# Hybrid SSD and Conformer layer: latent convolution in 32x32 tiles, layer norm by channels, decay rows on ScalarE's queue

## The chip, the cores and the metric

One Trainium2 core runs the whole program in one launch. Its engines work side by side and meet at semaphores: TensorE (PE, with PEld for its weight loads), VectorE (DVE), ScalarE (ACT), GpSimd (POOL) and SyncE (SP), which here only issues DMA transfers. The metric is the device time of one execution in microseconds (us).

## What is computed

One trunk layer is applied to 256 context tokens and to 2048 latent tokens (a grid of 32 rows by 64 columns), 1024 wide. After an RMS norm with a modulation, one projection gives all branches. The part that the change touches:

```python
h = ga * jax.nn.sigmoid(gb)
h = depthwise_conv(h, conv_w, conv_b)      # 31 taps along the grid's rows axis, per channel
h = layer_norm(h, ln_g, ln_b)              # over the 1024 channels of a token
y_conf = jax.nn.silu(h) * jax.nn.silu(gsil)
y_ssd = rms_norm((y_f + y_b + d * xs) * jax.nn.silu(z), norm_g)   # two scans, chunks of 128
out = jnp.concatenate([y_ssd, y_conf], -1) @ w_out
y = x + gate * rms_norm(out, g_post)
```

On the latent grid the convolution runs over the 32 rows for each of the 64 columns and each channel, so for one channel it is a 32x32 banded (Toeplitz) matrix times a 32x64 image. On the context it runs over 256 tokens.

## The kernel before

Activations are kept channel-major for the projection: 128 channels on partitions, tokens along the free axis. Float32 products of the projections are made of three passes of rounded halves (lines 378 to 380: high by high, low by high, high by low), 24 matmuls of 512 columns for one output bank of a block of 512 tokens. Three PSUM banks (`mm`) take these outputs in turn; five (`ss`) serve everything small. The 2304 tokens are worked in two halves (ten and eight tiles of 128 tokens). Each half first does the SSD inputs with their short convolution (`xbc_unit`), then `post`: the gated Conformer product (`gab_unit`, stored to DRAM as `GL`, channel-major), then the silu gates (`silu_unit`, stored to `ZS` and `GS`). Beside `post` runs a list of generators, `scan` and `extra`, which `interleave` and `merge` step at a fixed rate between the projection's matmuls.

- `scan` (`pass_a`, 18 tiles of 128 tokens) is the forward SSD scan. `load_lb` (line 664) loads rows of cumulated decays, spread over all partitions; POOL masks them (676), ACT takes the exponential (673, 684), DVE mixes the two directions (688, 689), and PE applies them (720). Each direction has four such buffers.
- `extra` in the second half holds the convolutions. `ctx_conv` does the context with 31 DVE steps, two PE transposes and a store to `CVC`. `lat_conv` does 128 latent channels: `kd` receives the banded taps, `x` the input, each in four loads. Four channels share one matmul: the partitions are 4 channels by 32 rows, and `expand` (line 622, ACT) writes the four 32x32 bands on the diagonal of a 128x128 weight. Channels are taken in eight groups of 128, and for each of them come four blocks of eight products (line 634), each block with one `ss` bank and one DVE instruction (639) that adds the bias. The result is stored token-major to `CVL` (644).

The last stage does the output projection, one tile of 128 tokens after another in the order 17 down to 2, then 1, 0. In tile i, 96 matmuls of 512 columns (`out_part`, line 1078) multiply the SSD half (`yh`, k = 0 to 7) and the Conformer half (`ph`/`pl`, k = 8 to 15) with `w_out`. Between them stand the preparations of later tiles. `ssd_pre` closes the backward scan for the tile after next (16 matmuls, 985) and squares it (989, 991). `ssd_norm` sums over the channels by a matmul with ones (1004), takes the root on POOL (135), and `ssd_scale` spreads it over the partitions by another matmul (1012, 1013). `conf_pre` loads the convolution token-major and takes mean and variance with DVE's statistics (1042 to 1047); `conf_act` transposes it back by eight PE transposes (1058), and applies the affine and silu on ACT (1061) and the gate on DVE (1063). `conf_hl` splits it in halves (1069, 1070). `finish` normalises the output, adds x and stores it.

The order of instructions on each engine is not simply that of the code: a planner replays the program with its own costs and, on each engine, takes the next instruction that its replay finds ready, by the order in the code. The result is fixed before the run. All DMA transfers are issued from SP's queue, in order, and a transfer that has to wait for a buffer holds those behind it.

Of the kernel before, what the change touches and what calls it, by code (L numbers as in the profile page):

```python
# [8 lines left out]
F32 = mybir.dt.float32  # L9
# [58 lines left out]
def backbone_kernel(ctx, tc, xa, xt_in, cols, rows, wconv, conf_b, gp_row, bg_row, state0, w_mod, w_dt, w_in, w_out,  # L68
# [19 lines left out]
    CVC = dram("cvc", [NCTX * P, D])  # L88
    CVL = dram("cvl", [LAT, D])
# [437 lines left out]

    def gab_unit(half, j, hb):
        wb = next_w()
        wa = next_w()  # L530
        for b in ORDER[half]:
# [48 lines left out]
    def ctx_conv(j, tile):  # L580
# [22 lines left out]
    def lat_conv(j, lp, kbuf):  # L603
        cbb = lp.tile([P, HD], F32, tag="cbb", name=f"cbb{j}", bufs=2)
        for h in range(2):
            c0 = j * P + h * 64
            DMA.dma_start(cbb[h * 64:(h + 1) * 64], conf_b[c0:c0 + 64].partition_broadcast(64))
        kd = lp.tile([P, 32, 32], F32, tag="kd", name=f"kd{j}", bufs=1)
        for c4 in range(4):
            src = bass.AP(tensor=wconv.tensor, offset=(j * 4 + c4) * 64 * 32, ap=[[32, 32], [1, 1024]])  # L610
            DMA.dma_start(kd[c4 * 32:(c4 + 1) * 32].rearrange("p r g -> p (r g)"), src)

        x = lp.tile([P, 32, 64], F32, tag="cx", name=f"cx{j}", bufs=1)
        src = GL[j][:, 256:].rearrange("(g c) (r w) -> c r g w", c=4, w=64)
        for c4 in range(4):
            DMA.dma_start(x[c4 * 32:(c4 + 1) * 32], src[c4])

        def expand(u):
            kt = kbuf[u % 2]
            for c4 in range(4):  # L620
                rs = slice(c4 * 32, (c4 + 1) * 32)
                S.copy(kt[rs, :, rs].rearrange("p (h q) r -> p h q r", h=2),
                       kd[rs].rearrange("p r (h u q) -> p u h q r", h=2, u=4)[:, u])

        vt = lp.tile([P, 32, HD], F32, tag="cvv", name=f"cvv{j}", bufs=1)
        yield
        expand(0)
        yield
        for u in range(4):
            kt = kbuf[u % 2]  # L630
            ps = bank("ss", f"cp{j}_{u}")
            for q in range(4):
                for h in range(2):
                    T.matmul(ps[h * 64:(h + 1) * 64, q * P:(q + 1) * P], x[:, h * 16 + u * 4 + q, :], kt[:, h * 4 + q, :],
                             start=True, stop=True)
            if u < 3:
                expand(u + 1)
            yield
            V.scalar_tensor_tensor(vt[:, ::-1, u * 16:(u + 1) * 16].rearrange("p r c -> p c r"),
                                   ps.rearrange("p (c r) -> p c r", r=32), 0.5,  # L640
                                   cbb[:, u * 16:(u + 1) * 16].unsqueeze(2).to_broadcast([P, 16, 32]), MUL, ADD)
        for h in range(2):
            c0 = j * P + h * 64
            DMA.dma_start(CVL[:, c0:c0 + 64].rearrange("(r w) c -> w r c", w=64), vt[h * 64:(h + 1) * 64])
        yield


    def pass_a(i):
# [11 lines left out]
        def load_lb(g, hq):  # L660
            for d in range(2):
                lb = pa.tile([P, 4, P], F32, tag=f"lb{d}", name=f"lb{i}{g}{hq}{d}", bufs=4)
                r0 = il * 32 + d * NH + g * 8 + hq * 4
                DMA.dma_start(lb.rearrange("p h l -> p (h l)"),
# [264 lines left out]
    kbuf = [lp.tile([P, 8, P], F32, name=f"kbuf{u}") for u in range(2)]  # L929
    for u in range(2):  # L930
        G.memset(kbuf[u], 0.0)
    blocks = post(1, 5)
    cg = lambda name: lp.tile([P, D], F32, tag="cg", name=name, bufs=2)
    extra = chain(f for j in range(4) for f in (lat_conv(2 * j, lp, kbuf), ctx_conv(j + 4, cg), lat_conv(2 * j + 1, lp, kbuf)))
# [32 lines left out]

    def ssd_pre(i, first):
# [21 lines left out]
        zr = p1.tile([P, P], F32, tag="zr", name=f"zr{i}", bufs=2)  # L990
        V.tensor_reduce(zr, z.rearrange("p q l -> p l q"), mybir.AxisListType.X, ADD)
# [9 lines left out]
    def ssd_norm(i, yz):  # L1001
        y, zr = yz
        pm = bank("ss", f"pm{i}")
        T.matmul(pm[:, 0:1], zr, ones[:, 0:1], start=True, stop=True)
        ms = p1.tile([P, 1], F32, tag="ms", name=f"yms{i}", bufs=2)
        V.tensor_scalar(ms, pm[:, 0:1], 1.0 / D, 4.0 * EPS, MUL, ADD)
        r = rstd_of(p1, ms, f"yr{i}")
        return y, r, pm

    def ssd_scale(i, yrp):  # L1010
        y, r, pm = yrp
        T.matmul(pm[:, P:2 * P], r.to_broadcast([P, P]), ident, start=True, stop=True)
        V.tensor_tensor(y, y, pm[:, P:2 * P].unsqueeze(1).to_broadcast([P, 8, P]), MUL)
        return ssd_hl(i, y)
# [22 lines left out]
    def conf_pre(i):  # L1037
        n = p2.tile([P, D], F32, tag="cn", name=f"cn{i}", bufs=1)
        DMA.dma_start(n, CVC[i * P:(i + 1) * P, :] if i < 2 else CVL[(i - 2) * P:(i - 1) * P, :])
        bs = p2.tile([P, 12], F32, tag="bs", name=f"bs{i}", bufs=2)  # L1040
        for h in range(2):
            V.bn_stats(bs[:, 6 * h:6 * h + 6], n[:, h * 512:(h + 1) * 512])
        mv = p2.tile([P, 2], F32, tag="mv", name=f"mv{i}", bufs=2)
        V.bn_aggr(mv, bs)
        V.tensor_scalar(mv[:, 1:2], mv[:, 1:2], EPS, None, ADD)
        r = rstd_of(p2, mv[:, 1:2], f"cr{i}")
        V.tensor_scalar(n, n, mv[:, 0:1], r, SUB, MUL)
        return n

    def conf_act(i, n):  # L1050
        gs = p2.tile([P, 8, P], F32, tag="gs", name=f"gsl{i}", bufs=1)
        DMA.dma_start(gs, chan_slice(GS, i))
        v = p2.tile([P, 8, P], F32, tag="v", name=f"v{i}", bufs=1)
        for g in range(2):
            ps = bank("ss", f"ct{i}{g}")
            for c in range(4):
                k = 4 * g + c
                T.transpose(ps[:, c * P:(c + 1) * P], n[:, k * P:(k + 1) * P], ident)
            for c in range(4):
                k = 4 * g + c  # L1060
                S.activation(v[:, k, :], ps[:, c * P:(c + 1) * P], AF.Silu, bias=cv[:, C_LNB + k:C_LNB + k + 1],
                             scale=cv[:, C_LNG + k:C_LNG + k + 1])
# [47 lines left out]
    gap(wo2, 64)  # L1110
# [8 lines left out]
    for b in range(2):  # L1119
        for n, u in enumerate(last):  # L1120
            run(take(u, 8))
            if b == 0 and n == 1:
                yr = ssd_norm(i, yz)
            if b == 1 and n == 0:
# [105 lines left out]
```

## Time and profile before

| | |
|---|---|
| time, median of 3 runs | 1878.53 us (1878.14 to 1878.75) |
| the profiled execution | 1882.2 us, its span 1880.5 us |
| granted TensorE clock | 0.986 of full speed |
| PE busy | 1825.6 us (97%) |
| DVE, ACT, POOL busy | 63%, 45%, 14% |
| DMA | 375.29 MB, 200 GB/s |

A group of the profile reads: line, engine, operation, output <- inputs, shape, count, then busy time in us and mean ns of one, then the idle time of that engine just before, with what ended it. Where a line is one of the timeline or of the chain of waits, it begins with its start in us. Float32 matmuls without the split into halves appear as two instructions each. A matmul's length contains its passage through the array; what one costs in a series is the distance between starts.

### The profile page before, as it was taken

What the parts mean: (1) busy time and instruction counts of PE and PEld (TensorE: products, weight loads), DVE (VectorE), ACT (ScalarE), POOL (GpSimd) and SP (SyncE); (2) the same over time, 40 slices, a digit from 0 to 9 for tenths busy, and PEclk for the clock granted to TensorE, in tenths of its full rate; (3) what the DMA queues carried; (4) which work ended last, traced back from release to release, by engine and by line L of the source; (5) the groups of instructions that cost most, each with busy time, mean ns of one, the idle gap of its engine ahead of it and who ended that gap; (6) DMA issues with size and microseconds to landing.
All of it is one profiled execution on the core that took longest, in us unless ns stands there. A gap on an engine that the chain in (4) does not pass through costs nothing.

```text
span 1880.5 us, 26833 instructions
## 1 busy us (share of the span) xinstructions
PE 1825.6 (97%) x9739; PEld 1504.6 (80%) x9739; DVE 1188.2 (63%) x1699; ACT 839.5 (45%) x1786; POOL 269.0 (14%) x351
## 2 busy tenths in 40 slices
PE   7899999999999999999999899999999999999998
PEld 4788887787887888888877677777887888888887
DVE  2477887776545553577585768655427676766662
ACT  3646424443455441644355666675414232232321
POOL 0002001111111100100001011110013333333220
PEclk9899999999999999999999999999999999999999
DMA  8556575564677754545587897978887655555532
GB/s 302 212 200 198 211 239 179 176 222 155 211 269 225 225 200 169 165 154 188 179 195 215 210 242 194 278 185 234 239 268 239 191 174 173 165 172 173 175 102 78
DMA packets 290400, 375.29 MB, mean 200 GB/s; under 512 B 85206, under 2 KB 187478, under 8 KB 290268
## 3 DMA queue, kind: packets, MB, share of 16 engines
q1 hardware_dynamic: 290268, 373.58, 64.2%
q8 instruction: 77, 1.26, 0.3%
q14 instruction: 55, 0.45, 0.1%
HBM read 243.92 MB, written 129.59 MB: 199 GB/s over the span
## 4 chain that ended last, share of the span: by engine, by line
PE 62%; DMA 5%; ACT 3%; issue 3%; DVE 2%; SPq 2%; POOL 0%; POOLq 0%; DVEq 0%; ACTq 0%
PE op L1078 20%; PE sp L378 6%; PE sp L379 6%; PE sp L380 6%; DMA lb<-lt 3%; PE xp L379 2%; PE xp L378 2%; PE xp L380 2%; PE py L720 2%; PE ga L378 2%; PE ga L380 1%; PE po L727 1%; PE ga L379 1%; PE qo L985 1%; PE gb L378 1%
## 5 line engine op out<-in xcount | busy, mean ns | idle before, releaser
L684 ACT ACTIVATE lb<-lb,WB 128x128 f32<-128x128 f32 x576 | 184.1, 391 | 150.9 <-POOL lb L676 149.0
L378 PE MATMUL sp<-hh,wh 128*128 128x512 f32 (+1 forms) x640 | 239.7, 375 | 2.6 <-DVE sth L550 2.6
L379 PE MATMUL sp<-hl,wh 128*128 128x512 f32 (+1 forms) x640 | 237.0, 370 | 0.0
L380 PE MATMUL sp<-hh,wl 128*128 128x512 f32 (+1 forms) x640 | 236.7, 370 | 0.2 <-DMA wl<-wld 0.2
L676 POOL TENSOR_SCALAR_AFFINE_SELECT lb<-lb 128x512 f32<-128x512 f32 x144 | 108.7, 760 | 749.7 <-ACT el L673 416.1
L378 PE MATMUL xp<-hh,wh 128*128 128x512 f32 (+1 forms) x480 | 179.1, 375 | 6.1 <-ACT wh L353 4.0
L379 PE MATMUL xp<-hl,wh 128*128 128x512 f32 (+1 forms) x480 | 179.1, 373 | 0.2 <-DVE hl L299 0.2
L380 PE MATMUL xp<-hh,wl 128*128 128x512 f32 (+1 forms) x480 | 179.2, 374 | 0.0
L475 DVE SCALAR_TENSOR_TENSOR cva<-raw,cwh,cva 128x1280 f32<-128x1280 f32 (+1 forms) x96 | 142.7, 1495 | 15.5 <-ACT cva L469 13.6
L378 PEld LDWEIGHTS sp<-hh,wh 128*128 128x128 f32 x640 | 121.0, 189 | 24.3 <-DVE sth L550 3.1
L380 PEld LDWEIGHTS sp<-hh,wl 128*128 128x128 f32 x640 | 121.0, 189 | 21.6 <-DMA wl<-wld 0.7
L379 PEld LDWEIGHTS sp<-hl,wh 128*128 128x128 f32 x640 | 121.2, 189 | 20.1 <-issue 0.5
L378 PE MATMUL gb<-hh,wh 128*128 128x512 f32 (+1 forms) x320 | 121.9, 381 | 3.4 <-DVE gth L539 3.4
L378 PE MATMUL ga<-hh,wh 128*128 128x512 f32 (+1 forms) x320 | 120.4, 376 | 2.6 <-ACT gth L536 2.6
L379 PE MATMUL gb<-hl,wh 128*128 128x512 f32 (+1 forms) x320 | 119.3, 373 | 0.0
L380 PE MATMUL gb<-hh,wl 128*128 128x512 f32 (+1 forms) x320 | 119.1, 372 | 0.0
L380 PE MATMUL ga<-hh,wl 128*128 128x512 f32 (+1 forms) x320 | 118.1, 369 | 0.0
L379 PE MATMUL ga<-hl,wh 128*128 128x512 f32 (+1 forms) x320 | 117.9, 369 | 0.0
L590 DVE SCALAR_TENSOR_TENSOR cg<-cg,cv 128x256 f32<-128x256 f32 x240 | 113.3, 497 | 2.5
L550 DVE SCALAR_TENSOR_TENSOR sth<-sth,sp 128x512 f32<-128x512 f32 (+1 forms) x80 | 50.4, 630 | 98.4 <-ACT sth L549 98.4
L378 PEld LDWEIGHTS xp<-hh,wh 128*128 128x128 f32 x480 | 92.0, 192 | 23.0 <-ACT wh L353 4.8
L688 DVE TENSOR_TENSOR lb<-lb,lb 128x512 f32<-128x512 f32 x72 | 51.6, 717 | 85.6 <-ACT lb L684 55.8
(219 smaller groups left out, 3860.8 us busy)
## 6 DMA issues: line engine op xcount, KB each, us to landing
lb<-lt SPq DMA_DIRECT2D x144, 256.0 KB, 4.2
wr<-in_w_in SPq DMA_DIRECT2D x88, 256.0 KB, 4.9
whd<-wh SPq DMA_DIRECT2D x44, 512.0 KB, 3.4
wld<-wl SPq DMA_DIRECT2D x44, 512.0 KB, 4.7
wh<-whd SPq DMA_DIRECT2D x44, 512.0 KB, 5.2
wl<-wld SPq DMA_DIRECT2D x44, 512.0 KB, 5.6
xT<-xb SPq DMA_DIRECT2D x18, 512.0 KB, 5.4
yp<-yg SPq DMA_DIRECT2D x36, 256.0 KB, 4.5
```

The lines of the kernel that those rows point to most:

```text
L378: T.matmul(ps[:, :BN], wh[:, k, :], hh[:, k, :], start=(k == 0), stop=False)
L379: T.matmul(ps[:, :BN], wh[:, k, :], hl[:, k, :], start=False, stop=False)
L380: T.matmul(ps[:, :BN], wl[:, k, :], hh[:, k, :], start=False, stop=(k == KT - 1))
L475: V.scalar_tensor_tensor(a[:, :n], raw[:, t:t + n], cwh[:, ct * 5 + t:ct * 5 + t + 1], a[:, :n], MUL, ADD)
L550: V.scalar_tensor_tensor(th, th, 1.0, ps[:, :BN], ADD, MUL)
L590: V.scalar_tensor_tensor(acc, g[:, t:t + 256], cv[:, w0 + t:w0 + t + 1], acc, MUL, ADD)
L676: G.affine_select(E[g, hq, d], E[g, hq, d], pattern=[[0, 4], [sg, P]], compare_op=ALU.is_ge, fill=NEG, base=0, channel_multiplier=-sg)
L684: S.activation(lb[:, h, :], lb[:, h, :], AF.Exp, bias=WB[:, i, c + h:c + h + 1])
L688: V.tensor_tensor(a, a, E[g, hq, 1], ADD)
L720: T.matmul(py[g][j * HD:(j + 1) * HD, q * P:(q + 1) * P], xt[g][:, h * HD:(h + 1) * HD], E[g, hq, 0][:, t, :], start=True, stop=True)
L727: T.matmul(po[g][:, q * P:(q + 1) * P], Sf[g][:, q * P:(q + 1) * P], bc[:, 2 + g, :], start=True, stop=True)
L1078: T.matmul(pso[n], lhs[:, k % 8, :], w[:, n * 512:(n + 1) * 512], start=(k == 0 and m == 0), stop=(k == 15 and m == 2))
```

## The change

Three things change together. The latent convolution is done in 32x32 tiles of the PE array: the bands themselves are the weights (`kt`), one channel per product, with 64 columns; in each half of `lat_conv` two row tiles (`a`) and four column tiles (`u`) are used, for two PSUM banks. The expansion into block-diagonal weights and its buffers go; one ACT copy per channel group remains, which turns the band and reorders it. Taps and input have two buffers, and `lat_load` fetches the next group when its gated product is already written. The bias comes in one table for all groups.

The convolution's result is stored channel-major for both passes (`CV`). The layer norm therefore works by channels: the mean is a sum over eight channel groups on DVE (`sum8`) and a matmul with ones; the variance is a square on ACT, `sum8`, and a matmul with ones together with that of the SSD norm (`norms`); one `spread` distributes both roots. The mean is taken two tiles ahead. The reduction over z (991) becomes `sum8` too. The context convolution loses its transposes.

The scan's decay rows are issued by ACT instead of SP.

```diff
+        if half:
+            gl_done.add(j)
...
-        ps = bank("ss", f"cps{j}")
-        for t in range(2):
-            T.transpose(ps[:, t * P:(t + 1) * P], acc[:, t * P:(t + 1) * P], ident)
         o = g[:, 768:1024]
-        S.mul(o, ps[:, :256], 0.5)
-        DMA.dma_start(CVC[:, j * P:(j + 1) * P].rearrange("(t p) c -> p t c", p=P),
-                      o.rearrange("p (t c) -> p t c", c=P))
-        yield
-    def lat_conv(j, lp, kbuf):
...
+        S.mul(o, acc, 0.5)
+        DMA.dma_start(CV[j * P:(j + 1) * P, 0:256], o)
+    def lat_load(j, lp):
+        kd = lp.tile([P, 32, 32], F32, tag="kd", name=f"kd{j}", bufs=2)
+        x = lp.tile([P, 32, 64], F32, tag="cx", name=f"cx{j}", bufs=2)
+        lat_in[j] = kd, x
+        for a in range(4):
+            rs = slice(a * 32, (a + 1) * 32)
+            src = bass.AP(tensor=wconv.tensor, offset=(j * 4 + a) * 64 * 32, ap=[[32, 32], [1, 1024]])
+            DMA.dma_start(kd[rs].rearrange("p r g -> p (r g)"), src)
+            DMA.dma_start(x[rs], GL[j][:, 256:].rearrange("(g a) (r w) -> a r g w", a=4, w=64)[a])
+    def lat_conv(j, lp, cbb, more):
+        if j not in lat_in:
+            lat_load(j, lp)
+        kd, x = lat_in.pop(j)
+        yield
+        kt = lp.tile([P, 32, 32], F32, tag="kt", name=f"kt{j}", bufs=1)
+        S.copy(kt[:, :, ::-1].rearrange("p g r -> p r g"), kd)
+        if more(j + 1):
+            lat_load(j + 1, lp)
+        yield
+        vt = lp.tile([P, 32, 64], F32, tag="cvv", name=f"cvv{j}", bufs=1)
         for h in range(2):
...
+            ps = {a: bank("ss", f"cp{j}_{a}") for a in (2 * h, 2 * h + 1)}
+            for q in range(8):
+                for u in range(4):
+                    for a in ps:
+                        rs = slice(a * 32, (a + 1) * 32)
+                        T.matmul(ps[a][u * 32:(u + 1) * 32, q * 64:(q + 1) * 64], kt[rs, u * 8 + q, :], x[rs, u * 8 + q, :],
+                                 start=True, stop=True)
+            yield
+            for a in ps:
+                V.scalar_tensor_tensor(vt[:, a::4, :], ps[a].rearrange("p (c w) -> p c w", w=64), 0.5,
+                                       cbb[:, j, a::4].unsqueeze(2).to_broadcast([P, 8, 64]), MUL, ADD)
+            yield
         for u in range(4):
...
+            c0 = j * P + u * 32
+            DMA.dma_start(CV[c0:c0 + 32, 256:].rearrange("c (r w) -> r c w", w=64), vt[u * 32:(u + 1) * 32])
...
-                DMA.dma_start(lb.rearrange("p h l -> p (h l)"),
+                S.dma_start(lb.rearrange("p h l -> p (h l)"),
                               LT[half][r0:r0 + 4, :].rearrange("h l -> (h l)").partition_broadcast(P))
...
+    def sum8(out, t, v):
+
+        V.tensor_tensor(t, v[:, 0:4, :], v[:, 4:8, :], ADD)
+        V.tensor_tensor(t[:, 0:2, :], t[:, 0:2, :], t[:, 2:4, :], ADD)
+        V.tensor_tensor(out, t[:, 0, :], t[:, 1, :], ADD)
+        return out
...
-        V.tensor_reduce(zr, z.rearrange("p q l -> p l q"), mybir.AxisListType.X, ADD)
+        zr = sum8(p1.tile([P, P], F32, tag="zr", name=f"zr{i}", bufs=2), z[:, 0:4, :], z)
...
+    def norms(i, yz, nq):
+
         pm = bank("ss", f"pm{i}")
...
+        src = [(c, e, t[1]) for c, e, t in ((0, 4.0 * EPS, yz), (1, EPS, nq)) if t]
+        for c, e, t in src:
+            T.matmul(pm[:, c:c + 1], t, ones[:, 0:1], start=True, stop=True)
...
+    def spread(i, rs):
+        pb = bank("ss", f"pn{i}")
+        for c, r in rs:
+            T.matmul(pb[:, c * P:(c + 1) * P], r.to_broadcast([P, P]), ident, start=True, stop=True)
+        return pb
...
+    def conf_load(i):
+        n = p2.tile([P, 8, P], F32, tag="cn", name=f"cn{i}", bufs=2)
+        DMA.dma_start(n, CV[:, i * P:(i + 1) * P].rearrange("(c p) t -> p c t", p=P))
         return n
...
+    def conf_mean(i, n):
+        t = p2.tile([P, 4, P], F32, tag="cs", name=f"cs{i}", bufs=1)
+        t = sum8(t[:, 0, :], t, n)
+        mean = bank("ss", f"cm{i}")[:, 0:P]
+        T.matmul(mean, ones, t, start=True, stop=True)
+        V.scalar_tensor_tensor(n, rows8(mean), -1.0 / D, n, MUL, ADD)
+        return n
+
+    def conf_square(i, n):
+        v = p2.tile([P, 8, P], F32, tag="v", name=f"v{i}", bufs=1)
+        S.activation(v, n, AF.Square)
+        return v, sum8(p2.tile([P, P], F32, tag="nq", name=f"nq{i}", bufs=2), v[:, 0:4, :], v)
+
+    def conf_act(i, n, v, pb):
         gs = p2.tile([P, 8, P], F32, tag="gs", name=f"gsl{i}", bufs=1)
         DMA.dma_start(gs, chan_slice(GS, i))
...
+        V.tensor_tensor(n, n, rows8(pb[:, P:2 * P]), MUL)
+        for k in range(8):
+            S.activation(v[:, k, :], n[:, k, :], AF.Silu, bias=cv[:, C_LNB + k:C_LNB + k + 1],
+                         scale=cv[:, C_LNG + k:C_LNG + k + 1])
...
         pt = conf_hl(i, v)
         banks(i)
...
         if not last:
+            v, nq = conf_square(nxt, n)
+        out_part(pso[i], yh, 0, 2)
+        if not last:
+            rs = norms(nxt, yz, (v, nq))
+        y = yz[0]
         if a + 2 < NT:
+            n2 = conf_load(order[a + 2])
             yz = ssd_pre(order[a + 2], order[a + 2] == NCTX - 1)
+        out_part(pso[i], yh, 2, 6)
         if not last:
+            pb = spread(nxt, rs)
+            yhn = ssd_scale(nxt, y, pb)
+        out_part(pso[i], yh, 6, 8)
+        out_part(pso[i], pt, 8, 9)
         if not last:
+            v = conf_act(nxt, n, v, pb)
+        out_part(pso[i], pt, 9, 11)
+        if a + 2 < NT:
+            n = conf_mean(order[a + 2], n2)
```

The prologue of the last stage follows the same steps for its first tile, one after the other, and two filler tiles of SBUF go.

More of the change, by code (lines that the diff above doesn't have):

```diff
@@ L87, in backbone_kernel @@
     GS = [dram(f"gs{h}", [D, HT[h] * P]) for h in range(2)]
-    CVC = dram("cvc", [NCTX * P, D])
-    CVL = dram("cvl", [LAT, D])
+    CV = dram("cv", [D, NT * P])
     YP = [dram(f"yp{i}", [P, D]) for i in range(NT)]
@@ L526, in xbc_phase @@
             pass
+    gl_done = set()
     def gab_unit(half, j, hb):
@@ L928, in backbone_kernel @@
     lp = ph_l.enter_context(tc.tile_pool(name="lp", bufs=1, side="right"))
-    kbuf = [lp.tile([P, 8, P], F32, name=f"kbuf{u}") for u in range(2)]
-    for u in range(2):
-        G.memset(kbuf[u], 0.0)
+    cbb = lp.tile([P, 8, 32], F32, name="cbb")
+    for u in range(4):
+        DMA.dma_start(cbb[u * 32:(u + 1) * 32],
+                      conf_b.rearrange("(j u n) -> u j n", u=4, n=32)[u].partition_broadcast(32))
     blocks = post(1, 5)
     cg = lambda name: lp.tile([P, D], F32, tag="cg", name=name, bufs=2)
-    extra = chain(f for j in range(4) for f in (lat_conv(2 * j, lp, kbuf), ctx_conv(j + 4, cg), lat_conv(2 * j + 1, lp, kbuf)))
+    lat = lambda j: lat_conv(j, lp, cbb, gl_done.__contains__)
+    extra = chain(f for j in range(4) for f in (lat(2 * j), ctx_conv(j + 4, cg), lat(2 * j + 1)))
     sc_ = scan(range(9, NT))
@@ L999, in ssd_pre, with ssd_scale @@
         return y, zr
-    def ssd_norm(i, yz):
-        y, zr = yz
-        pm = bank("ss", f"pm{i}")
[L1004 to L1014, printed above, removed]
+    rows8 = lambda t: t.unsqueeze(1).to_broadcast([P, 8, P])
+    def ssd_scale(i, y, pb):
+        V.tensor_tensor(y, y, rows8(pb[:, 0:P]), MUL)
+        return ssd_hl(i, y)
+    def norms(i, yz, nq):
+        pm = bank("ss", f"pm{i}")
+        src = [(c, e, t[1]) for c, e, t in ((0, 4.0 * EPS, yz), (1, EPS, nq)) if t]
+        for c, e, t in src:
+            T.matmul(pm[:, c:c + 1], t, ones[:, 0:1], start=True, stop=True)
+        rs = []
+        for c, e, t in src:
+            ms = p1.tile([P, 1], F32, tag=f"ms{c}", name=f"yms{i}{c}", bufs=2)
+            V.tensor_scalar(ms, pm[:, c:c + 1], 1.0 / D, e, MUL, ADD)
+            rs.append((c, rstd_of(p1, ms, f"yr{i}{c}")))
+        return rs
+    def spread(i, rs):
[3 more added lines that the diff above has]
+        return pb
     def ssd_hl(i, y):
@@ L1035, in load_gg @@
         gg[a] = t
[L1037 to L1047, printed above, removed]
-        return n
@@ L1119, in backbone_kernel @@
     for b in range(2):
[L1120 removed]
+        for m, u in enumerate(last):
             run(take(u, 8))
[L1122 to L1124 removed]
+            if b == 0 and m == 1:
+                rs = norms(i, yz, None)
+            if b == 1 and m == 0:
+                yh = ssd_scale(i, yz[0], spread(i, rs))
                 ph_b[1].close()
                 p2 = ph_1.enter_context(tc.tile_pool(name="p2", bufs=1))
[L1127 to L1129 removed]
+                n = conf_mean(i, conf_load(i))
     for u in last:
         run(u)
[L1132 removed]
+    v, nq = conf_square(i, n)
+    v = conf_act(i, n, v, spread(i, norms(i, None, (v, nq))))
     ph_b[2].close()
@@ L1140, in backbone_kernel @@
     yz = ssd_pre(order[1], False)
+    n = conf_mean(order[1], conf_load(order[1]))
     for a, i in enumerate(order):
```

70 lines of the change are left out of this document (5 added, 65 removed).

## The prediction

> **What bounds the kernel now.** I read the page first, then the stretches by stage, then PE's waits, then single stretches of the timeline.
>
> ```profile
> span 1880.5 us, 26833 instructions
> PE 1825.6 (97%) x9739; PEld 1504.6 (80%) x9739; DVE 1188.2 (63%) x1699; ACT 839.5 (45%) x1786; POOL 269.0 (14%) x351
> ```
>
> ```profile
> 300.00:600.00 300.00, 291.32 (x1642) 243.67 (x1642) 196.19 (x361) 142.99 (x364) 36.83 (x57) 0.99 0.63 206
> 950.00:1060.00 110.00, 104.87 (x610) 81.65 (x609) 86.60 (x161) 62.99 (x143) 11.78 (x18) 0.97 0.79 199
> 1060.00:1345.00 285.00, 272.68 (x1652) 214.20 (x1651) 178.07 (x270) 181.17 (x407) 30.76 (x46) 0.98 0.83 226
> 1480.00:1840.00 360.00, 360.00 (x1776) 303.23 (x1775) 245.39 (x289) 103.73 (x216) 113.42 (x97) 1.00 0.53 164
> ```
>
> Columns: stretch, length, then busy time of PE, PE's weight loads, DVE, ACT, POOL, then PE's clock, DMA share and GB/s. PE bounds every stage. The output stage (1480 to 1840) leaves it no idle time at all, so there only PE instructions saved can shorten anything. The latent convolution stands between 950 and 1345, where PE idles 5.1 + 12.3 us. Nearly all of that has one owner:
>
> ```profile
> L634 PE MATMUL cp<-kbuf,cx 128*64 128x128 f32 x512 | 37.1, 291 | 12.4 <-ACT kbuf L622 10.0 <-DMA cx<-gl 1.9 <-DVE cvv L639 0.3
> L622 ACT COPY kbuf<-kd 32x256 f32<-32x256 f32 x128 | 83.3, 657 | 19.6 <-DMA kd<-in_wconv 11.8 <-PE cp L634 6.0
> ```
>
> PE waits 12.2 us for ACT's expansion of the taps into block-diagonal weights and for the input. So the change can win by giving PE less to execute, by removing these 12.2 us, and by little else.
>
> **The latent convolution on PE.** One of today's 32 blocks, in the timeline (start, length, count):
>
> ```profile
> 1327.29 0.39 PE L378 MATMUL sp<-hh,wh 128*128 128x512 f32 x1
> 1327.52 0.39 PE L379 MATMUL sp<-hl,wh 128*128 128x512 f32 x1
> 1327.75 0.39 PE L380 MATMUL sp<-hh,wl 128*128 128x512 f32 x1
> 1328.07 1.09 PE L634 MATMUL cp<-kbuf,cx 128*64 128x128 f32 x16
> 1329.09 0.50 PE L378 MATMUL sp<-hh,wh 128*128 128x512 f32 x1
> 1329.43 0.40 PE L379 MATMUL sp<-hl,wh 128*128 128x512 f32 x1
> ...
> 1328.06 0.85 PEld L634 LDWEIGHTS cp<-kbuf,cx 128*64 128x64 f32 x16 [0.35 <-issue]
> ```
>
> Projection matmuls start every 0.227 us. Between 1327.75 and 1329.43 two such steps (0.45) are due, so the block costs 1.68 − 0.45 = 1.23 us: 0.86 of 16 matmuls (8 products, two instructions each) and 0.37 of draining into and out of the narrower array shape. 32 blocks are 39.4 us.
>
> The change makes 16 blocks of 64 products, so 128 matmuls of 64 columns in 32x32 tiles, each with its own weight load. What decides is how many run at once. Three rows tell:
>
> ```profile
> 1533.86 1.78 PE qo L985 x16
> 1539.74 0.22 PE pm L1012 x2
> ...
> 23.14 2.13 PE L239 MATMUL mp<-wm,sc 128*2 128x256 f32 x32
> ```
>
> On the whole array a 128-column float32 matmul takes 1.78/16 = 0.111 us. The block above does the same length at 0.86/16 = 0.054, so its two column tiles overlap fully. The modulation's four column tiles take 2.13/32 = 0.067 for 256 columns, where 0.222 would be due: about four at once, loads included. Sixty-four columns are 0.056 us. With four column tiles at once, which is shown, a new block is 128 × 0.056 / 4 = 1.78 us; with the two row tiles of a block also at once, which nothing in this trace shows, 0.89. I take the middle, 1.33. With the same 0.37 of draining: 16 × 1.70 = 27.2 us, a gain of 12.2 (ends: 20.2 and 34.4 us, gains of 19.2 and 5.0). What speaks against it is the number of instructions: 16 loads and 16 matmuls in 0.86 us are 27 ns an instruction, and no row shows PE taking a long series faster. That is a rival below.
>
> **The waits of that stage.** The 128 expansions go; one copy per channel group (L622's successor, strided) replaces sixteen. At 1.06 us (ACT's 1024-element square, below) to 4 × 0.657 = 2.63 us, eight cost 8.5 to 21 us against 83.3. Taps and input are double-buffered and loaded a group ahead, but only once the gated product of the next group is stored, which I expect to fail for the first two of eight groups. So 12.2 × 6/8 = 9.2 us go; bounds 0 and 12.2. Against it: a block now holds two of the five small PSUM banks until two 1.06-us DVE instructions have emptied them, so scan matmuls behind it on PE can wait. DVE's lateness costs PE 0.3 us there today; I take 0, and at most 16 × 1.06 = 17 us.
>
> **Decay rows on ACT's queue.** 144 loads move past SP's queue into ACT's instruction stream.
>
> ```profile
> L664 SPq DMA_DIRECT2D lb<-lt x144: 319/360/2937, 152.2 to 1291.4; - x144
> ...
> SPq L664 <- DVE lb L688: 117.5, 43, 8.6
> ...
> POOL lb L676 <- DMA lb<-lt: 267.4, 57, 14.0
> ```
>
> Each issue takes 0.36 us, so ACT spends 144 × 0.36 = 52 us, half in the latent stage, where it loses over 60 of expansions, half in the first scan, where it was busy 143 of 300 us. The buffer waits (117.5 us, longest 8.6) come along. Behind a waiting load on ACT stand the scan's exponentials and the tanh that frees a projection bank. There are three such banks of 24 matmuls (24 × 0.227 = 5.4 us), so PE has 10.9 us of other banks before it stops; 8.6 fits in that. In return rows arrive sooner for POOL, which waits 267 us, but PE lost only 8.7 us in the first scan. I take 0, with ±8.7 us.
>
> **The context convolution** drops two transposes per channel group: 16 × 0.109 (0.87/8 below) = 1.7 us off PE. Its stores and the latent ones, 32 instead of 16 in 256-byte pieces as before, lie beside PE's work.
>
> **The output stage.** One tile today, by the chain of waits:
>
> ```profile
> 1520.46 0.87 PE ct L1058 x8
> 1521.33 9.56 PE op L1078 x42
> ...
> 1545.45 0.87 PE ct L1058 x8
> ```
>
> A tile takes 24.99 us. The eight transposes (0.87) go. Three pairs come: the mean (two, 0.22 as L1012's), a second column sum (0.22 at most), a second spread (0.22). PE saves 0.21 per tile, 17 × 0.21 = 3.6 us. On DVE:
>
> ```profile
> L991 DVE TENSOR_REDUCE zr<-z 128x128 f32<-128x1024 f32 x18 | 36.2, 2011 | 1.1 <-ACT z L989 1.1
> L1042 DVE BATCH_NORM_STATS2 bs<-cn 128x6 f32<-128x512 f32 x36 | 23.2, 685 | 19.9 <-DMA cn<-cvl 19.3 <-DMA cn<-cvc 0.6
> L1047 DVE TENSOR_SCALAR cn<-cn,mv,cr 128x1024 f32<-128x1024 f32 x18 | 14.6, 813 | 11.1 <-POOL cr L135 11.1
> L1013 DVE TENSOR_TENSOR y<-y,pm 128x1024 f32<-128x1024 f32 x18 | 21.8, 1209 | 2.9 <-PE pm L1012 2.9
> L688 DVE TENSOR_TENSOR lb<-lb,lb 128x512 f32<-128x512 f32 x72 | 51.6, 717 | 85.6 <-ACT lb L684 55.8 <-issue 18.9 <-POOL lb L676 4.9
> L305 DVE TENSOR_TENSOR ht<-ht,pr 128x256 f32<-128x256 f32 x8 | 2.7, 417 | 0.0
> L989 ACT ACTIVATE z<-y 128x1024 f32<-128x1024 f32 x18 | 19.1, 1062 | 144.9 <-DVE y L988 144.8
> ```
>
> Out: 2.01 + 2 × 0.69 + 0.81 = 4.2. In: three eight-to-one sums of three adds each (0.72 + 0.42 and about 0.28 by halving the step again = 1.42, so 4.26) and two full-width instructions at 1.21: 6.7. DVE grows by 2.5 us of 25, from 245/360 = 68% to 78%; ACT gains one square of 1.06. Both stay off the bound. New is a dependence inside the tile. The convolution's square may overwrite its buffer only when the low-half subtraction of the tile before has read it:
>
> ```profile
> 1579.36 0.62 PE L1078 MATMUL op<-woh,yh 128*128 128x512 f32 x2
> ...
> 1580.19 1.23 DVE L1070 TENSOR_TENSOR pl<-v,ph 128x1024 fp32r<-128x1024 f32 x1 [1.22 <-ACT ph L1069]
> ...
> 1582.66 1.41 DVE L1094 SCALAR_TENSOR_TENSOR o<-op,or,gg 128x512 f32<-128x512 f32 x2 [0.92 <-POOL or L135]
> ```
>
> The tile starts at 1579.36; the square can start at 1581.42, its sum is done at 1581.42 + 1.06 + 1.42 = 1583.9. The column sums stand in the code behind 12 matmuls, at 1579.36 + 2.72 = 1582.1: PE would be there 1.8 us early, and 4.4 us early if DVE first does the 1.41 above and the residual addition (1.23). PE's order is the planner's, though, and it already puts other matmuls ahead of late ones:
>
> ```profile
> 1440.76 0.39 PE L1078 MATMUL op<-woh,pl 128*128 128x512 f32 x1
> 1441.05 0.65 PE L1058 MATMUL ct<-ident,cn 128*128 128x128 f32 x4
> 1441.46 0.47 PE L1078 MATMUL op<-woh,pl 128*128 128x512 f32 x1
> ```
>
> Twenty-four more output matmuls (5.4 us) can fill. I charge 0.3 us for each of 16 tiles, 5 us in all; bounds 0 and 71.
>
> At the change of stages the first tile's norm becomes a chain without cover: square 1.06, sum 1.42, two PE pairs 0.44, POOL's root 0.55, a 1.21 product, some 4.7 us, against 0.87 of transposes gone. PE stands 3.6 us there today for late weights:
>
> ```profile
> PE op L1078 <- ACT woh L961: 2.2, 1, 2.2
> PE op L1078 <- DVE wol L962: 1.4, 1, 1.4
> ```
>
> The two delays overlap in part; I charge 3 us (0 to 4.7).
>
> **Sum:** −12.2 − 9.2 + 0 − 1.7 − 3.6 + 5 + 3 = −18.7 us. The profiled execution took 1882.2 us, span 1880.5, 0.2% above the median 1878.53; from the median the sum gives **1860 us**.
>
> **Rivals.**
> - *PE takes instructions no faster than today's block* (27 ns each): 256 × 27 ns = 6.9 us per block, 16 × 7.3 = 116 us instead of 27.2, and 1949 us. For it: no row is faster over a long series. Against: four tiles' matmuls and loads share 0.27 us in the modulation, a length that their columns alone explain.
> - *One matmul start per 27 ns*, loads hidden: 128 × 27 ns = 3.46 us, 16 × 3.83 = 61 us, and 1894 us. It turns slower when a block passes about 2.9 us (16 × 1.17 eats the 18.7). The Trainium skill, "TensorE: Matmul & The Clock Gate", section "Wait — 56ns, not 53.3ns?", says that starts never come closer than about 25 ns; with that figure the estimate is 16 × 3.57 = 57 us, about 1890. The same page's "Part 3: Packing small matmuls — row/col tiling" has tiles starting some 4 ns apart and sixteen at 10.6 times one, which would be near the 0.89 end, 1853. The trace settles neither for 64 columns.
> - *The column sums wait on PE in every tile.* Place: behind the first 12 matmuls of each output tile. Price 1.8 to 4.4 us, 16 × 1.8 = 29 to 71 us in place of 5: 1884 to 1926 us. It decides from (18.7 + 5)/16 = 1.5 us a tile. The moved transposes above speak against it, the fixed place in the code for it.
> - *The waits only change their name:* 9.2 us stay and the bank holding or ACT's loads cost 9 more: about 1878, no change.
> - *Everything at its good end:* 7 more from the row tiles, 3 from waits, 5 from the column sums: about 1845.
>
> **Chances:** forecast 0.56, better end 0.08, no change 0.07, column sums 0.11, start floor 0.10, instruction rate 0.08. Within 0.2% (3.8 us, about what a measurement can tell here) I put 0.07, faster 0.64, slower 0.29. The forecast's own range is 1847 to 1876; with the better end, the column sums' lower part and the start floor it is 1842 to 1902.
>
> **What would show it.** The row of the convolution's matmuls: 2048 of 32x32, in blocks of about 1.3 us (0.9: row tiles overlap; 3.5 or 7: a rival). PE's waits: no row for the expansion. The output tile's period: 24.8 us if right, 26.6 or more if the column sums wait. PE's idle time from 300 to 600 no longer than 8.7 us if ACT's loads are harmless. A block over 2.9 us, or a tile over 26.1, makes the forecast wrong.

## The result, and the profile after

The changed kernel takes **1922.83 us** (1917.61 to 1925.88) against 1878.64 us (1878.14 to 1880.33) for the kernel before beside it: 1.0231 times, 95% interval 1.0207 to 1.0254. The forecast was 1860, in a range of 1842 to 1902. Two rows of the page of the kernel after, busy time and share of its span:

```profile
span 1921.1 us, 29715 instructions
PE 1827.8 (95%) x11223; PEld 1506.3 (78%) x11223; DVE 1207.8 (63%) x1807; ACT 799.6 (42%) x1684; POOL 267.0 (14%) x349
```

The span grows by 40.6 us, PE's busy time by only 2.2, so PE mostly stands still longer. To see where, I take two marks that both kernels have: the last input product (`xp`, where the second half's gate products and the latent convolution begin) and the last gate product (`sp`, where the output products take over). The groups of these tiles, with first and last start, before and then after:

```profile
L380 PE MATMUL xp<-hh,wl x480: 278/389/783, 38.2 to 917.1; 128*128 128x512 f32 x134, 128*128 128x256 f32 x26
L380 PE MATMUL sp<-hh,wl x640: 278/389/628, 509.6 to 1419.5; 128*128 128x512 f32 x128, 128*128 128x256 f32 x32
```

```profile
L379 PE MATMUL xp<-hh,wl x480: 278/389/631, 38.8 to 913.9; 128*128 128x512 f32 x134, 128*128 128x256 f32 x26
L379 PE MATMUL sp<-hh,wl x640: 277/389/476, 511.0 to 1402.1; 128*128 128x512 f32 x128, 128*128 128x256 f32 x32
```

The stage with the latent convolution went from 502.4 to 488.2 us: **14.2 us won**. The first output tile (from its first output product to the next tile's) went from 32.1 to 41.9 us, and the 16 tiles behind it from 24.77 to 27.98 us on average: 9.8 + 51.4 = **61 us lost**. The other 6 us of the difference lie outside these marks: 3.2 ahead of the last `xp` (which lies between 908.8 and 920.5 in the traces of all the kernels here), 2.6 between the last gate product and the first output product, 0.4 at the end. In the windows by stage of the kernel after, the output stage that had no idle time now has 26.7 us of it, and a lower clock:

```profile
950.00:1060.00 110.00, 100.17 (x1105) 78.56 (x1104) 100.84 (x199) 48.38 (x120) 16.21 (x21) 0.97 0.87 216
1060.00:1345.00 285.00, 277.92 (x2746) 221.17 (x2745) 157.84 (x239) 136.17 (x321) 33.20 (x43) 0.99 0.84 239
1480.00:1840.00 360.00, 333.34 (x1559) 278.78 (x1557) 239.91 (x331) 108.72 (x205) 97.40 (x88) 0.96 0.55 151
```

So of 360 us, 26.7 are idle and about 0.04 × 360 = 14 are lost to the clock; these 41 us are what the 12.9 tiles of this window take longer. PE's waits over the whole run (total, times, longest) name one owner above all, the next tile's SSD half, `yh` and `yl`:

```profile
PE op L1093 <- ACT yh L1035: 26.1, 10, 5.3
...
PE op L1093 <- ACT ph L1084: 5.2, 1, 5.2
...
PE op L1093 <- DVE yl L1036: 4.7, 2, 2.4
...
PE pm L1018 <- DVE nq L972: 2.8, 1, 2.8
```

For the column sums themselves (`pm`) PE waits once in the whole run. Why `yh` is late shows in the chain of waits of the kernel after, around the start of one tile (start, length, what):

```profile
1673.72 17.07 PE op L1093 x68
1690.79 0.12 PE pm L1018 x2
1690.91 5.12 PE op L1093 x22
1696.02 0.22 PE pn L1029 x2
1696.24 0.24 PE cm L1062 x2
1696.48 0.02 issue
1696.51 1.22 DVE cn L1063
1697.73 1.14 DVE y L1010
1698.87 0.02 issue
1698.89 1.05 ACT yh L1035
1699.94 0.04 issue
1699.98 1.61 PE op L1093 x4
```

The column sum of the squares (`pm`) stands behind 68 output products (the chain leaves out the tile's first four), not behind 12 as in the code; 22 more follow before the spread `pn`. The `pn` in the chain carries the SSD norm's root, and the one that follows it in PE's order carries the Conformer's. After the second spread PE has two output products left in this tile (none to 26 in the others), while the next tile needs, one after the other, the mean subtraction of the tile two ahead (`cn`, 1.22, which DVE has in its order ahead of `y`), the scaling of `y` (1.14) and the rounding (1.05). That is 3.7 us from 1696.24 to 1699.98, and most of it is a hole on PE.

In this tile no engine had made the sum late. The sum of squares that `pm` needs (`nq`) was done on DVE at 1684.4, and DVE then stood idle until PE came to `pm`, whose result DVE reads next:

```profile
1690.94 0.22 DVE L1022 TENSOR_SCALAR yms<-pm 128x1 f32<-128x1 f32 x2 [5.83 <-PE pm L1018]
```

It is PE's fixed order that puts sum and spread at the end of the tile. Whether an earlier place in that order alone would have been enough was not tried.

The hole is paid twice. Windows around another one, with the granted clock in the third column from the end:

```profile
1860.00:1862.00 2.00, 2.00 (x12) 1.59 (x11) 0.17 (x1) 0.79 (x3) 0.00 (x0) 1.00 0.00 0
1862.00:1865.30 3.30, 0.02 (x1) 0.00 (x0) 3.30 (x4) 1.52 (x3) 0.00 (x0) 0.86 0.00 0
1865.30:1868.70 3.40, 3.39 (x9) 2.81 (x10) 2.74 (x7) 3.19 (x8) 0.55 (x1) 0.50 0.00 0
1868.70:1871.20 2.50, 2.50 (x7) 1.92 (x7) 2.50 (x3) 1.05 (x1) 0.00 (x0) 0.50 0.59 175
```

After 3.3 us without matmuls the next 5.9 us run at 0.50 of full speed, which costs 3 us more. Of the other holes behind the first tile, eight are followed by one slow stretch of 3.4 us, which costs 1.7, and three by none.

### The profile page after: what moved, and what is told of

Same layout as the page of the kernel before. It is cut to its first block, busy times and chain, and to the rows that moved or that the text cites. A ratio compares the mean times of both kernels' runs of the same rounds, so it can differ in the third digit from the quotient of the medians.

```text
span 1921.1 us, 29715 instructions
## 1 busy us (share of the span) xinstructions
PE 1827.8 (95%) x11223; PEld 1506.3 (78%) x11223; DVE 1207.8 (63%) x1807; ACT 799.6 (42%) x1684; POOL 267.0 (14%) x349
## 4 chain that ended last, share of the span: by engine, by line
PE 82%; DMA 6%; DVE 6%; issue 3%; ACT 2%; POOL 0%; SPq 0%; POOLq 0%; DVEq 0%; ACTq 0%
PE op L1093 18%; PE sp L377 7%; PE sp L378 7%; PE sp L379 7%; PE xp L377 5%; PE xp L378 5%; PE xp L379 5%; PE ga L377 3%; PE ga L379 3%; PE ga L378 3%; PE gb L377 3%; PE gb L379 3%; PE gb L378 3%; PE py L718 2%; PE po L725 2%
## 5 line engine op out<-in xcount | busy, mean ns | idle before, releaser
L1093 PE MATMUL op<-woh,yh 128*128 128x512 f32 x288 | 95.7, 410 | 26.3 <-ACT yh L1035 26.1
L594 DVE SCALAR_TENSOR_TENSOR cg<-cg,cv 128x256 f32<-128x256 f32 x240 | 107.8, 489 | 0.6
```

Of the source, the lines that this page charges most:

```text
L594: V.scalar_tensor_tensor(acc, g[:, t:t + 256], cv[:, w0 + t:w0 + t + 1], acc, MUL, ADD)
L1093: T.matmul(pso[n], lhs[:, k % 8, :], w[:, n * 512:(n + 1) * 512], start=(k == 0 and m == 0), stop=(k == 15 and m == 2))
```

## The experiments

**The tie between the two norms.** `norms` sums both in one bank, and one `spread` serves both, so the SSD norm, whose sum is ready early, stands behind the Conformer's.

```diff
-            rs = norms(nxt, yz, (v, nq))
+            rs = norms(nxt, yz, None)
...
-            pb = spread(nxt, rs)
-            yhn = ssd_scale(nxt, y, pb)
+            yhn = ssd_scale(nxt, y, spread(nxt, rs))
+            rc = norms(nxt, None, (v, nq))
...
-            v = conf_act(nxt, n, v, pb)
+            v = conf_act(nxt, n, v, spread(nxt, rc))
```

> The changed kernel with the two norms taken apart again: the SSD half's column sum, root and spread have their own PSUM bank and stand before those of the convolution. Nothing else is changed. Theory 1 (the joint norm ties the next tile's SSD half to the convolution's variance, so its rounded half is late and PE waits 2 to 3 us at the start of each output tile and then runs at half clock for 3.4 us): the output tiles go from 28.8 back to about 25 us, PE's wait for that half (26 us) goes, and the time falls by 40 to 50 us to about 1875. Theory 2 (DVE's added work, or the loop through the one buffer of the convolution's values, is too long for 25 us): tiles stay at 28 us or more, the wait moves to the Conformer half, and the time stays above 1905.

Measured: 1909.95 us (1902.71 to 1916.93), 1.0147 times the kernel before (1.011 to 1.0185), the time of theory 2. The wait for `yh` fell from 26.1 to 5.8 us, but PE now waits 13.4 us for the low half `pl` and 8.1 for `ph`. DVE's timeline of this kernel shows who holds `pl` up:

```profile
1578.02 0.69 DVE L970 TENSOR_TENSOR cs<-cn 128x512 f32<-128x512 f32 x1 [2.19 <-DMA cn<-cv]
1578.63 1.22 DVE L1085 TENSOR_TENSOR pl<-v,ph 128x1024 fp32r<-128x1024 f32 x1
```

`pl` is needed by the tile that runs; ahead of it in DVE's fixed order stands the mean of the tile two ahead, which waits 2.19 us for its load.

**The decay rows back on SyncE's queue** (one word: `S.dma_start` to `DMA.dma_start` in `load_lb`).

> The changed kernel with the decay rows issued by SyncE again. Theory 1 does not touch it: the output stage stays as it is, the time moves by less than 9 us either way (1913 to 1931), as ACT's 144 issues of 0.36 us and their waits are covered by PE's work. Rival: ACT's issues delay the tanh that frees PE's banks (5.2 us of idle PE at 1085 us, 3.7 at 364), then the first scan and the latent stage get 9 us shorter or more.

Measured: 1928.53 us, 1.0246 times (1.0221 to 1.0271). The queue move did not make the kernel slow; that it helps, and where, shows further down.

**The tie between tiles.** The squares go to the gate's buffer `gs`, so they do not wait until the low-half subtraction of the tile before has read `v`.

```diff
-        v = p2.tile([P, 8, P], F32, tag="v", name=f"v{i}", bufs=1)
+        v = p2.tile([P, 8, P], F32, tag="gs", name=f"vq{i}", bufs=1)
         S.activation(v, n, AF.Square)
```

> The changed kernel with the convolution's squares written into the gate's buffer instead of the buffer of the convolution's values, so that the square no longer waits until the tile before has been split into halves. Theory 1 (joint norm): the joint sums still stand late in PE's order, tiles stay at 27 to 29 us, the time within 12 us of the changed kernel. Theory 2 (the loop through that one buffer): the loop gets about 4 us shorter, tiles come near 25 us and the time falls by 30 us or more.

Measured: 1908.92 us, 1.0144 times (1.0119 to 1.017), 13.9 us won, a little more than theory 1 allows and half of what theory 2 asks for. Tiles alternate between about 26 and 28 us, and PE still waits 26.4 us for `yh`. The buffer is a part of the loop, not the whole.

**The decay rows on ACT's queue, nothing else changed.**

> The kernel before with only the decay rows issued by ScalarE. If the queue is covered by PE's work: within 9 us of before, 1870 to 1888. If ACT's waits for free buffers stop PE: 10 to 25 us slower, seen as longer PE idle time between 300 and 600 and between 950 and 1345 us. If earlier rows end PE's stalls there: up to 9 us faster.

Measured: 1883.67 us, 1.0006 times (0.9988 to 1.0024): no change, as forecast for this part by itself.

**Both ties cut at once.**

> Both edits of the two runs before at once: the SSD norm has its own bank and spread, and the Conformer's squares go to a buffer that no half-subtraction reads. Theory (the two ties between tiles are all that makes a tile long): the two gains of 12.9 and 13.9 us add, 1923 - 27 = 1896 us or, if nothing else is in the way, tiles of 25 to 25.5 us and 1870 to 1876. Rival (with the mean of the tile two ahead standing in VectorE's order before the half-subtraction, the wait only moves on): tiles stay at 26 to 27.5 us and the time at 1905 to 1912.

Measured: 1894.95 us, 1.0075 times (1.0058 to 1.0092). The gains add up, 28 us for the two against 13 and 14, but tiles still take 24.3 to 29.6 us, 26.3 on average. PE's waits and a piece of DVE's timeline:

```profile
PE op L1094 <- DVE pl L1086: 12.5, 10, 2.2
```

```profile
1609.48 1.21 DVE L1079 SCALAR_TENSOR_TENSOR v<-v,gsl 128x1024 f32<-128x1024 f32 x1
1610.62 2.29 DVE L995 TENSOR_TENSOR y<-y,z 128x1024 f32<-128x1024 f32 x1
1612.83 0.68 DVE L970 TENSOR_TENSOR cs<-cn 128x512 f32<-128x512 f32 x1
1613.44 1.21 DVE L1086 TENSOR_TENSOR pl<-v,ph 128x1024 fp32r<-128x1024 f32 x1
```

Between the multiplication by the gate that finishes `v` and the subtraction that makes `pl`, DVE has work of the tile two ahead in its order. I read this as the silu of a tile still coming so late that any such work shows on PE; no run tested it by itself.

**The whole norm two tiles ahead.** Squares and their column sum follow the mean at once, in a buffer of their own; inside the tile only scaling and silu are left.

```diff
+    rc = norms(order[1], None, conf_square(order[1], n))      # before the loop
...
-            v, nq = conf_square(nxt, n)
...
-            rs = norms(nxt, yz, (v, nq))
+            rs = norms(nxt, yz, None)
...
-            pb = spread(nxt, rs)
+            pb = spread(nxt, rs + rc)
...
             n = conf_mean(order[a + 2], n2)
+            rc = norms(order[a + 2], None, conf_square(order[a + 2], n))
```

> The kernel after, with the Conformer's squares and their column sum also two tiles ahead, right behind the mean, in a buffer of their own; one spread takes both roots, the SSD norm's column sum stands alone. Theory (the loop square, sum, root, spread, scaling, silu within one tile makes the tiles long, and the clock is halved only because TensorE waits): tiles of 24.8 to 25.3 us, clock 1.00 in the output stage, and with 10 us still lost at the change of stages 1868 to 1876 us. Rival (VectorE's extra 2.5 us a tile or the order of its work keeps TensorE waiting wherever the sums stand): tiles of 27 us or more, 1905 or above.

Measured: **1871.91 us** (1870.21 to 1877.44), 0.9949 times the kernel before (0.9928 to 0.9969), half a per cent below it and 51 us below the changed kernel. All tiles but the first take 24.8 us or less. The window of the output stage and the chain of waits in it:

```profile
1480.00:1840.00 360.00, 360.00 (x1761) 303.35 (x1760) 271.68 (x375) 124.08 (x235) 122.09 (x97) 1.00 0.58 163
...
1681.69 1.89 PE qo L992 x16
1683.59 5.04 PE op L1094 x22
1688.62 0.44 PE pn L1029 x4
1689.07 5.48 PE op L1094 x24
1694.54 0.22 PE cm L1062 x2
1694.77 5.26 PE op L1094 x23
```

PE is never idle although DVE does more than before (271.7 us of 360 against 245.4): not DVE's amount of work made the tiles long, but the chain of sum, root, spread and scaling that stood at the end of each. Both roots are spread (`pn`, four instructions) with at least 47 output products (24 and 23) between them and the next tile.

**Ten matmuls more in each tile.** They write a bank that nobody reads and stand just ahead of the wait for `yh`.

```diff
+            fl = bank("ss", f"fl{a}")
+            for _ in range(10):
+                T.matmul(fl, WH[0][:, 0:P], WL[0][:, 0:512], start=True, stop=True)
             yh = yhn
```

> The kernel after, with ten more 512-column matmuls at the end of each of the first 17 output tiles, into a bank that nobody reads: 2.27 us of TensorE's work a tile just ahead of its wait for the next tile's SSD half. It changes no result. Theory (a wait of 2 to 3 us costs its own length and then 1.5 to 2.5 us of half clock): the added work lies in the wait, the clock stays full, and the time falls by 16 times 1.5 to 2.5, less what overfills: 1885 to 1905 us. Rival 1 (the loop through ScalarE and VectorE sets the tile's length and the half clock hides in it): 1919 to 1927. Rival 2 (TensorE's own work is the bound): 1923 + 36 = 1959.

Measured: 1906.66 us (1904.59 to 1909.1), 1.0137 times (1.0119 to 1.0155): 17 × 2.27 = 39 us more work, 16 us less time than the kernel after, and just above the theory's 1905. The output stage's window:

```profile
1480.00:1880.00 400.00, 399.91 (x1928) 334.94 (x1927) 270.80 (x375) 127.42 (x241) 100.35 (x93) 1.00 0.51 146
```

No idle time and full clock; a tile takes 27.1 us on average, that is 24.8 + 2.27. With 2.27 us more to do on PE, tiles are 0.9 us shorter than the 27.98 without. A wait that is only filled cannot do that, a clock that stays up can. The planner's order is not quite the same in the two: with the filling, 7 or 8 output products follow the last spread in most tiles, without it none to 26. But where 7 or 8 follow without it, the holes are still 2.1 to 2.4 us (those that begin at 1523.8 and 1639.0), and the mean is 26.7 / 12.9 = 2.1, so the order is not what won. The second price of the wait is shown.

**The latent convolution alone.** The kernel before with the 32x32 tiles, but storing by tokens as before, and everything else as before:

```diff
-    def lat_conv(j, lp, kbuf): ...
+    def lat_conv(j, lp, cbb, more): ...                       # as in the change
+        vt = lp.tile([P, 64, 32], F32, tag="cvv", name=f"cvv{j}", bufs=1)
+            DMA.dma_start(CVL[:, c0:c0 + 32].rearrange("(r w) c -> r w c", w=64), vt[u * 32:(u + 1) * 32])
```

> The kernel before with the latent convolution in 32x32 tiles alone: output stage, layer norm, context convolution and decay rows as before; the result is stored by tokens in pieces of 128 bytes (256 before). Theory (the latent part won what the trace shows, 17.4 us at the last gate matmul, of which 1.7 are the context's transposes, and all loss is in the output stage): 1861 to 1867 us, last gate matmul near 1404, output tiles 25.0 us. Rival (the gain only postpones a wait, or the shorter pieces slow the stores that the first output tiles read): 1874 to 1882.

Measured: 1911.51 us, 1.0158 times (1.0138 to 1.0178). Output tiles are 25.0 us, so the loss of the change is indeed in its layer norm; but the latent stage, instead of winning, took 538.7 us. Both theories fail. ACT's waits there, and the issues on SyncE's queue during the longest of them:

```profile
ACT el L674 <- DMA lb<-lt: 92.7, 19, 18.1
...
1054.01 6.85 SPq L617 DMA_DIRECT2D kd<-in_wconv  x4
1060.95 0.37 SPq L665 DMA_DIRECT2D lb<-lt  x1
1061.42 4.95 SPq L618 DMA_DIRECT2D cx<-gl  x4
1068.94 0.81 SPq L665 DMA_DIRECT2D lb<-lt  x2
```

Decay rows (`lb`) stand behind the taps and inputs of the next group, which are loaded early and wait for their buffers; the scan stops.

**The same with the decay rows on ACT's queue.**

> The kernel before with the latent convolution in 32x32 tiles, stored by tokens, and now with the decay rows on ScalarE's queue; all else as before. Theory (in the run without it the decay rows stood on SyncE's queue behind the latent loads, ScalarE waited 92.7 us for them and longest 18.1, and that cost 32 us): last gate matmul at 1402 to 1412, 1863 to 1875 us. Rival (the 128-byte pieces and VectorE's strided writes, 1.09 us against 0.68, cost it): last gate matmul at 1440 or later, 1900 or above.

Measured: 1903.08 us, 1.0111 times (1.0087 to 1.0135); the latent stage takes 523.1 us. The time and the last gate product (1440.8) are those of the rival. The queue gave back 15.6 us in that stage, half of the 32 that the theory put on it; 35 us against the kernel after remain. DVE waits 30.3 us in all (longest 12.0) there for a store of the scan, 15.0 (4.8) in the kernel after:

```profile
DVE yg L757 <- DMA yp<-yg: 30.3, 7, 12.0
```

**Strided writes, stores as in the change.** The kernel with the norm two ahead, where DVE writes tokens outermost (1.10 us instead of 0.68 each) and the stores stay in 256-byte pieces.

> The run with both column sums two tiles ahead, where VectorE writes the latent result with tokens outermost (stride 32, as the store by tokens needs it) but the stores stay as they are, 256-byte pieces by channel; the latent values so land in a scrambled order, and the layer norm works on other numbers. Theory S (VectorE's strided writes, 1.09 us against 0.68, 13 us over 32 instructions, cost the store by tokens its gain): last gate matmul near 1435, 1895 to 1905 us. Theory P (the 128-byte pieces of the stores, or the order that the planner makes of that kernel, cost it): last gate matmul at 1404 to 1412, 1870 to 1880.

Measured: 1877.5 us, 0.9983 times (0.9969 to 0.9996), latent stage 491.8 us, as without the strides. So DVE's strided writes are not what costs the store by tokens its gain. Left are its 128-byte pieces, the context's transposes with their copy on ACT, which that kernel still has, and the order that the planner makes of it; these were not told apart.

**The decay rows back on SyncE's queue, norm two tiles ahead.**

> The run with both column sums two tiles ahead, with the decay rows back on SyncE's queue. Theory (with the new latent loads on SyncE's queue, decay rows behind them come late): 6 to 12 us more than 1871.9, last gate matmul at 1411 to 1418 instead of 1405.6. Rival (the queue does not matter, as it did not in the kernel before): 1868 to 1876.

Measured: 1879.5 us, 0.9986 times (0.9971 to 1.0001), against 0.9949 with ACT's queue. The latent stage took 501.5 us, and 498.7 in the changed kernel with that edit; the eight kernels with the new convolution stored by channels and ACT's queue took 487.6 to 495.4. So the queue move is worth some 9 us of that stage beside the new loads, and nothing to speak of beside the old ones (500.6 against 502.4).

**The first tile earlier.** Mean, squares, sums and silu of the first tile between the last gate products, the second tile's norm inside the first tile.

```diff
-    v, nq = conf_square(i, n)
-    v = conf_act(i, n, v, spread(i, norms(i, None, (v, nq))))
+                rc = norms(i, None, conf_square(i, n))        # between the last gate units
+            if b == 1 and m == 1:
+                v = conf_silu(i, n, spread(i, rc))
...
+    v = conf_gate(v, gs)                                      # behind them
```

> The run with both column sums two tiles ahead, with the first output tile's norm started earlier: mean ahead of the SSD scaling, squares, sums and silu between the last gate products, only the gate behind them; the second tile's norm stands inside the first tile. Theory (the first tile's 47.7 us are the late norm chain of the first and second tile): 40 to 44 us for the first tile, the rest at 24.8, 1864 to 1868 us. Rival (the stored gates, 12 us from the last tanh to the product, and the last output weights set that stage anyway): first tile 46 us or more, 1870 to 1874.

Measured: 1875.93 us, 0.9969 times (0.9954 to 0.9984); the theory's 1864 to 1868 is missed. The first tile fell from 47.7 to 41.8 us, but the second rose from 24.8 to 27.9. That is 69.7 us for the two, against 72.4; yet the two kernels above that have the output stage unchanged from the version two tiles ahead took 69.4 (decay rows on SyncE's queue) and 70.3 (strided writes). So no gain is shown, and the change of stages stays open.

## Why the prediction was wrong

**What bounds the kernel: right.** PE bounds each stage, and the output stage had no slack. This is why the loss there is complete: nothing else could absorb a late half tile.

**The latent convolution on PE: right.** One block of the kernel after, in the timeline:

```profile
1124.14 0.39 PE L378 MATMUL gb<-hl,wh 128*128 128x512 f32 x1
1124.37 0.39 PE L379 MATMUL gb<-hh,wl 128*128 128x512 f32 x1
1124.69 1.48 PE L634 MATMUL cp<-cx,kt 32*32 32x64 f32 x128
1126.10 0.50 PE L377 MATMUL ga<-hh,wh 128*128 128x512 f32 x1
1126.44 0.40 PE L378 MATMUL ga<-hl,wh 128*128 128x512 f32 x1
```

By the prediction's own method it costs 1126.44 − 1124.37 − 0.45 = 1.62 us, where 1.70 was forecast: 25.9 us for 16, a gain of 13.5. Fourteen of the 16 cost this; the two at 1025 and 1035 us took 4.44 and 3.54, with waits of 1.85 and 1.58 us inside and a falling clock. Without the 0.37 of draining, 128 matmuls and 128 loads take 1.25 us (from the first start to the last it is 1.26). That lies between the 1.78 of four column tiles at once and the 0.89 with the row tiles too, so the two row tiles overlap in part, and at 4.9 ns an instruction both issue rivals fall. That the middle, 1.33, came so close was luck; it was chosen for want of a row. The Trainium skill's floor of about 25 ns between starts ("TensorE: Matmul & The Clock Gate", "Wait — 56ns, not 53.3ns?") does not hold between different tiles of the array here, where a start comes each 9.8 ns on average.

**The waits of that stage (−9.2): wrong.** PE's waits for the expansion are gone, but the two windows from 950 to 1345 hold 9.8 + 7.1 = 16.9 us of idle time after and 5.1 + 12.3 = 17.4 before. The largest wait there now is 5.7 us for projection weights from DMA (`wh`), and 3.5 us lie inside the two long blocks. So the first half of the rival, that the waits only change their name, was right. The 12.2 us that the prediction gave to the latent products were also only 70% of the 17.4, not nearly all. What the stage won, 14.2 us in one trace, is within 1 us of the blocks and the transposes, 13.5 + 1.7, but that closeness is partly luck: the same stage took 487.6 to 495.4 us in the eight traces above.

**The decay rows (0 ± 8.7): right by themselves, wrong beside the new loads.** Priced alone, they change nothing, and PE's idle time from 300 to 600 us is 7.9 us after and 8.3 with this part alone, below the 8.7 that the prediction set as the sign of harm. The prediction did not ask what the loads a group ahead do to the queue that the decay rows would have stayed on; there the move is worth 9 us. Without it the new convolution wins about 2 us of the stage (500.1 on average of two against 502.4).

**The output stage's amounts: right.** The tile of the version with the norm two ahead takes 24.8 us (25.0 − 0.21 forecast), and DVE grows by 26.3 us in 360, some 1.8 a tile (2.5 forecast).

**"I charge 0.3 us for each of 16 tiles": this is the step that failed.** Measured is 3.2 us a tile, and as that is net of the 0.21 saved, the cost is 3.4 a tile, 55 us instead of 5. (By the same sum a tile over 26.3, not 26.1, was the sign of a slower kernel.) It has three parts.
- I took from one row that the planner puts other matmuls ahead of late ones, and so fills. It does, and too well: it moved the sums behind some 70 output products instead of 12, and the spread to the end of the tile. Then PE does not wait at the sums (2.8 us in all) but at what hangs on them: 26.1 us for `yh`. I followed the wait at its place in the code and not what is late next.
- I followed the Conformer's norm alone. The change puts the SSD norm into the same bank and the same spread, so the half tile that is needed first waits for the one that is needed last; cutting that and the shared `v` buffer gave back 28 us, and moving the whole sum two tiles ahead 51, which leaves nothing of the loss in the tiles behind the first.
- I left the clock out. In the output stage it took about 14 of 41 us.

The rival "the column sums wait on PE in every tile" had the right size (1884 to 1926 us), got 0.11, and its place was off by a step in the same way.

**The change of stages (3 us): too small.** The first tile lost 9.8 us. PE waits in it 5.2 us for `ph` and 5.3 for `yh`, where it waited 3.6 for weights before. In the version with the norm two tiles ahead the first tile even takes 47.7 us, with 9.8 of waiting for `ph`. The prediction counted the first tile's chain alone, and not that the second tile's norm runs through the same engines at that time; that this is the cause is argued, not shown.

## What to carry to other kernels

When a reduction over partitions moves into a pipelined loop, follow its result to the consumer that is needed first, in the order in which the engines will really run, and count how many matmuls are left between the last link and that consumer; a wait that disappears at the sum can stand one tile on. Norms that are needed at different times are better not tied by one bank and one spread, and a norm that takes sum, root, spread and scaling cost nothing here once its sums stood a whole tile ahead of its use. A change that loads earlier on a shared queue has to be priced together with whatever else waits on that queue.

## What the runs showed of the hardware

Two to three microseconds without a matmul can halve the clock for the next 3.4. After the hole of 3.30 us quoted above 5.9 us ran at 0.50; in the 3.4 us after holes of 2.8 and 2.1 us (at 1697 and 1524) the mean was 0.58. It is not each hole, though. In this trace the slow stretches begin on a fixed grid with steps of 3.413 us (at 1615.21, 1642.52, 1673.24 and 1700.54, for instance, 8, 9 and 8 steps apart), wherever the hole itself lies. Two holes of 2.1 us, at 1613.3 and at 1730.2, in windows cut along that grid:

```profile
1611.80:1615.21 3.41, 1.19 (x4) 0.67 (x4) 3.41 (x5) 3.26 (x9) 3.41 (x4) 1.00 0.14 38
1615.21:1618.62 3.41, 3.17 (x8) 2.49 (x9) 2.97 (x4) 1.15 (x2) 2.81 (x2) 0.50 0.53 174
...
1727.84:1731.26 3.42, 1.96 (x11) 1.25 (x10) 3.42 (x5) 3.24 (x7) 3.40 (x4) 1.00 0.14 38
1731.26:1734.67 3.41, 2.37 (x10) 1.99 (x11) 3.22 (x3) 1.15 (x4) 3.41 (x2) 1.00 0.41 107
```

The first hole lies nearly whole in one step, which keeps 1.19 us of matmuls, and the next step runs at half speed. The second is split over two steps, which keep 1.96 and 2.37 us, and the clock stays up. In all fourteen traces, from 100 us on, a step at full clock with less than 1.47 us of matmuls was followed by a slow one each time, one with more than 2.1 us only once; in between both occur. The Trainium skill ("TensorE: Matmul & The Clock Gate", "What's actually happening") puts the fall to half speed behind an idle window of about 3.4 us and lets that window run freely, whatever the kernel does. The length of the slow stretch and the fixed grid agree with it; the window need not be idle as a whole here.

Sixty-four products in 32x32 tiles, two row tiles and four column tiles in turn, ran at 4.9 ns for each load or matmul over 256 of them, where the series of 16 in the kernel before took 27.
